# Moving keys, queries, a pool unit and a gate unit to other places of an attention loop that fills its waits with matmuls

## The chip, the cores and the metric

The kernel runs on one core of one Trainium2 chip. The metric is device time in microseconds (us) of one execution; lower is better. Five engines work beside one another, each in the order in which the program was written: PE (TensorE, matmuls), DVE (VectorE), ACT (ScalarE), POOL (GpSimd) and SP (SyncE, which here issues DMAs). An engine that waits for another one's result holds up all that is queued behind it on the same engine.

## The reference

One layer of an encoder trunk on 512 tokens of width 1024, in fp32:

```python
xn = rmsnorm(h, norm_mix[l])
proj = xn @ w_in[l]
u_s5, u_pool, qkv, gate_logits = jnp.split(proj, split_at, axis=-1)
y_s5 = s5_mixer(u_s5, ...)        # diagonal state space, both directions, GLU output
y_pool = pool_mixer(u_pool, ...)  # centred means over 2/4/8/16 tokens minus self, grouped linear
y_attn = dilated_attention(qkv)   # 16 heads of 64, three dilated windows merged, ALiBi
gates = jax.nn.sigmoid(gate_logits).reshape(bsz, L, N_BRANCHES, D_MODEL)
merged = (gates[:, :, 0] * (y_s5 @ w_branch_s5[l])
          + gates[:, :, 1] * (y_pool @ w_branch_pool[l])
          + gates[:, :, 2] * (y_attn @ w_branch_attn[l]))
h = h + merged @ w_out[l]
hn = rmsnorm(h, norm_mlp[l])
h = h + jnp.square(jax.nn.relu(hn @ w_up[l])) @ w_down[l]
```

A last rmsnorm follows. Queries, keys and values of all heads, the pool inputs and the gate logits are 128-column slices of the same product `xn @ w_in`, so they depend on nothing but the normed input and may be computed in many orders.

## The kernel before

**Matmuls.** Every large product is done with three matmuls of 128x512 per 128-row slice of the contraction: `mm3` (L121 to L123) multiplies the high part of a weight by the high and the low part of the input, and the low part of the weight by the high part of the input. A `unit_quanta` is one 128-column slice of output: 8 quanta of three matmuls into one PSUM bank (called `ps`), then a `done` function that takes the bank out. Weights arrive by DMA (`raw`), ACT rounds them to the high part `wh` (L96), and DVE subtracts for the low part `wl` (L103); this is done ahead, one unit at first and two in the stage after attention.

**Order.** Nothing reorders at run time. The order of each engine is that of the Python program: `tick()` is called after each quantum and runs what `later(n, f)` put off, and generators that `start` put in the background, which give a few instructions per tick. So where a unit stands in the list decides where all that hangs on it stands.

**Attention.** Nine steps i of eight slots s. In a slot PE does four transposes (L795) of the softmax output of head 2(i-1)+s//4, then one quantum of `main`, a tick, a second quantum of `main`, and the two score matmuls (L764, L765) of a row block of head 2i+s//4. `main` is other work that fills the time. Behind a score block DVE adds the bias and takes the maximum (L768), ACT takes the exponential (L775), and once per head DVE takes the reciprocals of the sums (L779) and POOL divides, four instructions (L109 on POOL, `S<-S,sm`). The transposes of a head need that division. `k_done` and `q_done` write a new key or query unit: two heads each, ACT copies and a DVE subtraction (L103 with 64x512 for a key, L106 for a query). POOL and DVE also make the weights of the S5 layer (`W_gen`, 64x64 matmuls at L832).

**The scan.** `s5_scan` is the S5 recurrence: 63 steps of four small POOL instructions (`st<-XS,A` twice, `st<-st`, `XS<-XS,st`). It starts in step 5, slot 3, of attention, and each step needs the one before it.

**After attention.** Stage C1 is eight rounds m of a gate unit (its `done` is a tanh on ACT, L1015) and a branch unit. At m = 6 (`V_UNIT`) `s5_script` starts: four ACT copies out of the scan's result (L96, `z<-XS`), products on DVE, four more copies and products, and then `kq`, 32 small matmuls at L1096, inside the gate unit of m = 7. The stages C2, C3, the output projection and the MLP follow.

The profile's L96, L103, L106 and L109 are helpers (`copy`, `tt`, `stt`, `ts`); the names of the tiles tell the uses apart.

Of the kernel before, what the change touches and what calls it, by code (L numbers as in the profile page):

```python
# [13 lines left out]
AF = mybir.ActivationFunctionType  # L14
# [41 lines left out]
def trunk(ctx: ExitStack, tc: tile.TileContext, a: dict, out):  # L56
    nc = tc.nc
    VE, SE, GE, TE, SP = nc.vector, nc.scalar, nc.gpsimd, nc.tensor, nc.sync
# [17 lines left out]
    def z(dt=F32, n=512):  # L76
        t = z_p.tile([128, 512], dt, tag="z", name="z")
        return t if n == 512 else t[:, 0:n]

    def zr():  # L80
        return z(F32R)

    def ps():
        return ps_p.tile([128, 512], F32, tag="ps", name="ps")
# [9 lines left out]
    def copy(eng, o, i, scale=1.0):  # L94
        if eng is SE:
            SE.activation(out=o, in_=i, func=AF.Copy, scale=scale)  # L96
        elif scale != 1.0:
            eng.tensor_scalar(out=o, in0=i, scalar1=scale, scalar2=1.0, op0=MUL, op1=MUL)
        else:
            eng.tensor_copy(out=o, in_=i)  # L100

    def tt(o, i, j, op, eng=None):
        (eng or VE).tensor_tensor(out=o, in0=i, in1=j, op=op)  # L103
# [15 lines left out]
    def mm3(o, wh, wl, xh, xl, first, last):  # L119

        TE.matmul(o, wh, xh, start=first, stop=False)  # L121
        TE.matmul(o, wh, xl, start=False, stop=False)  # L122
        TE.matmul(o, wl, xh, start=False, stop=last)  # L123
# [8 lines left out]
    def later(n, f):  # L132
        clock[1] += 1
        put_off.append((clock[0] + n, clock[1], f))

    def tick():
        clock[0] += 1
        due = sorted(x for x in put_off if x[0] <= clock[0])
        if due:
            put_off[:] = [x for x in put_off if x[0] > clock[0]]  # L140
            for _, _, f in due:
                f()
        for b in background:
            if b[0] <= clock[0]:
                try:
                    b[0] = clock[0] + (next(b[1]) or 1)
                except StopIteration:
                    b[0] = None
        background[:] = [b for b in background if b[0] is not None]
# [8 lines left out]
    def run(qs):  # L158
        for q in qs:
            q()  # L160
            tick()
# [7 lines left out]
    def add_piece(src, kind="w"):  # L169
        pieces.append((src, kind))  # L170
        if kind != "s":
            loaded.append(len(pieces) - 1)
        return len(pieces) - 1
# [61 lines left out]
    def use(i):  # L235

        j = i + 1
        while j < len(pieces) - 1 and pieces[j][1] == "z":
            j += 1
        d = SPLIT_AT  # L240
        if state["deep"] or "s" in [kind for _, kind in pieces[i:i + 3]]:
            j, d = i + 2, 1
        while state["split"] <= min(j, len(pieces) - 1):
            hi, lo = split_ops()
            later(d, hi)
            later(d + 1, lo)
            d += 3
        return splits[i]

    def cols(w, c0, n=128):  # L250

        return w[:, c0:c0 + n].rearrange("(k p) f -> p k f", p=128)
# [4 lines left out]
    w_in, w_out, w_up, w_down = a["w_in"], a["w_out"], a["w_up"], a["w_down"]  # L257
    C_POOL, C_Q, C_K, C_V, C_G = 512, 1024, 2048, 3072, 4096
# [2 lines left out]
           for hf in range(2)]  # L261
    P_s5 = [add_piece(cols(w_in, 128 * j)) for j in range(3)]
    P_qk = []
    for i in range(8):
        if i == 1:
            P_s5.append(add_piece(cols(w_in, 384)))
        P_qk.append((add_piece(cols(w_in, C_K + 128 * i)), add_piece(cols(w_in, C_Q + 128 * i))))
    P_pool = [add_piece(cols(w_in, C_POOL + 128 * j)) for j in range(4)]
    P_c1 = [(add_piece(cols(w_in, C_G + 2048 + 128 * m)), add_piece(cols(a["w_branch_attn"], 128 * m))) for m in range(8)]
    P_c2, P_c3 = [], []  # L270
    for lst, off, w in ((P_c2, 1024, a["w_branch_pool"]), (P_c3, 0, a["w_branch_s5"])):
        for m in range(0, 8, 2):
            g = [add_piece(cols(w_in, C_G + off + 128 * (m + i))) for i in range(2)]
# [24 lines left out]
    for x in range(8):  # L298
        i, hf = x // 2, x % 2
# [79 lines left out]
    xT_h, xT_l = [xh_[:, k] for k in range(8)], [xl_[:, k] for k in range(8)]  # L379
# [293 lines left out]
    def unit_quanta(pi, hT, lT, done, ks=range(8), sub=None):  # L673

        box = {}
        q = []
        n = len(ks)

        def quantum(i):
            if i == 0:  # L680
                box["w"] = use(pi)
                box["p"] = ps()
            hs, ls = box["w"]
            wh, wl = hs[i], ls[i]
            if sub is not None:
                wh, wl = wh[:, sub], wl[:, sub]
            mm3(box["p"], wh, wl, hT[ks[i]], lT[ks[i]], i == 0, i == n - 1)
            if i == n - 1:
                done(box["p"])

        return [lambda i=i: quantum(i) for i in range(n)]
# [31 lines left out]
    def k_done(i):  # L723
        def f(p):
            def part_(b):
                h = 2 * i + b
                u, o = slice(64 * b, 64 * b + 64), slice(64 - 64 * b, 128 - 64 * b)
                kh = khh[h] = zr()
                kl = kll[h] = kz[b][i % 2]
                copy(SE, kh[u], p[u])  # L730
                copy(SE, kh[o], p[u])
                later(1, lambda: tt(kl[u], p[u], fr(kh[u]), SUB))
            part_(0)
            later(2, lambda: part_(1))
        return f

    def q_done(i):
        def f(p):
            def part_(b):
                h = 2 * i + b  # L740
                u, o = slice(64 * b, 64 * b + 64), slice(64 - 64 * b, 128 - 64 * b)
                qs = qst[h] = zr()
                copy(SE, qs[u], p[u], 0.125)
                stt(qs[o], p[u], 0.125, fr(qs[u]), MUL, SUB)
            part_(0)
            later(2, lambda: part_(1))
        return f
# [56 lines left out]
    def av(i):  # L804

        p = ps()
        for kt in range(4):
            for b in range(2):
                h = 2 * i + b
                c = h % 8 * 64  # L810
                TE.matmul(p[64 * b:64 * b + 64], vt[kt][h // 8][:, c:c + 64], pts.pop((h, kt)),  # L811
                          start=kt == 0, stop=kt == 3)
        h, l = yT_h[i], yT_l[i] = zr(), zr()
        copy(SE, h, p)
        later(1, lambda: tt(l, p, fr(h), SUB))
# [46 lines left out]
    def pool_u_done(g):  # L862
        def f(p):
            upool.append(z())
            copy(SE, upool[g], p)
        return f
# [85 lines left out]
    qs = unit_quanta(P_s5[3], xT_h, xT_l, s5_u_done(3))  # L952
# [6 lines left out]
    load_T(1)  # L959
    W_load(0)  # L960
    run(qs[4:])
    for i in range(9):
        main = []
        if i < 7:
            main += unit_quanta(P_qk[i + 1][0], xT_h, xT_l, k_done(i + 1))
            main += unit_quanta(P_qk[i + 1][1], xT_h, xT_l, q_done(i + 1))
        else:
            for g in (0, 1) if i == 7 else (2, 3):
                main += unit_quanta(P_pool[g], xT_h, xT_l, pool_u_done(g))
        for s in range(8):  # L970
            if s % 4 == 0:
                W_load(2 * i + s // 4 + 1 - W_DELAY)
                W_ops(2 * i + s // 4 - W_DELAY)
            if 2 * i + s // 4 == 8 + W_DELAY and s % 4 == 3:
                start(s5_scan())
            if i >= 1:
                t_quantum(2 * (i - 1) + s // 4, s % 4)()
            main[2 * s]()
            tick()
            main[2 * s + 1]()  # L980
            if i < 8:
                s_quantum(2 * i + s // 4, s % 4)()
                if s in (3, 7) and 2 * i + 2 + s // 4 < H:
                    load_T(2 * i + 2 + s // 4)
            if s in (2, 6):
                W_mm(2 * i + s // 4 - 1 - W_DELAY)
            if s == 2 and i >= 2:
                av(i - 2)
            tick()
    av(7)  # L990
    att_p.release()
    kz_p.release()
# [13 lines left out]
    acc = {}  # L1006
    w3_p = tc.alloc_tile_pool(name="w3", bufs=1, side="right", reuse_waits="tile")
    state["wide"], state["deep"] = w3_p, True

    def gate(pi):  # L1010
        box = {}

        def done(p):
            box["th"] = z()
            SE.activation(out=box["th"], in_=p, func=AF.Tanh, scale=0.5)  # L1015
        return box, unit_quanta(pi, xT_h, xT_l, done)

    def branch_done(box, m, stage):
        def f(p):
# [224 lines left out]
    for m in range(8):  # L1244
        if m == V_UNIT - 1:
            V_load(0)
        if m == V_UNIT:
            start(s5_script())
        box, qs = gate(P_c1[m][0])
        run(qs)  # L1250
        run(unit_quanta(P_c1[m][1], yT_h, yT_l, branch_done(box, m, 0)))

    for stage, P, yh, yl in ((1, P_c2, ypool_h, ypool_l), (2, P_c3, ys_h, ys_l)):
        for n, (gs, b) in enumerate(P):
# [3 lines left out]
            for pi in gs:  # L1258
                box, qs = gate(pi)
# [68 lines left out]
    for t in range(4):  # L1328
# [3 lines left out]
        p = tok_inner(P_wo[1], mh, ml, t, mid)  # L1332
# [183 lines left out]
    for t in range(3):  # L1516
        p = tok_inner(P_dn3[1], aT_h, aT_l, t)
# [15 lines left out]
    for q in range(2):  # L1533
        p = ps()
# [91 lines left out]
```

## Time and profile before

| what | value |
|---|---|
| median of 3 runs | 942.47 us (941.71 to 943.56) |
| the profiled execution, its own time | 941.8 us |
| its span, first to last instruction | 940.0 us |
| PE busy | 918.0 us, 98% |
| DVE, ACT, POOL busy | 585.0 us (62%), 444.7 us (47%), 307.5 us (33%) |
| mean granted TensorE clock | 0.994 of full speed |

The profile is of one execution whose own time is 941.8 us; 1.8 us of that lie outside the span. Its times are given in microseconds from the start of the span. An idle time in a row is the time that the engine stood still before the instruction; "<-" names the engine, tile and line that ended the wait.

### The profile page before, as it was taken

To read this page: it belongs to the slowest core of one execution; us is meant where nothing else is said; L and a number is where in the kernel's file an instruction comes from. 1 tells how busy PE (TensorE), PEld (TensorE's weight loads), DVE (VectorE), ACT (ScalarE), POOL (GpSimd) and SP (SyncE) were. 2 spreads that over 40 slices of the span, in tenths; PEclk is the share of its full clock that TensorE was granted. 3 is DMA by queue.
4 is the path that set the end of the run, shared out by engine and by line. 5 is a ranking of instruction groups with operands and counts; after the bars stand their busy time and mean duration, and the time that the engine had idled before them with its cause. 6 is when DMAs were issued, how large, how long until landed. Compare 5 with 4: busy or idle time off the path is not lost.

```text
span 940.0 us, 12763 instructions
## 1 busy us (share of the span) xinstructions
PE 918.0 (98%) x4683; PEld 736.2 (78%) x4683; DVE 585.0 (62%) x921; ACT 444.7 (47%) x711; POOL 307.5 (33%) x416
## 2 busy tenths in 40 slices
PE   8999999999999999999989999999999999999997
PEld 6778777677777888887878888888888888888876
DVE  4698787886645655668554454436665857675443
ACT  5544765566654324555333233346444444444522
POOL 0000466556788882021010000056134314511302
PEclk9999999999999999999989999999999999999999
DMA  9237766633213334444512245271333124221222
GB/s 327 80 120 200 202 181 179 164 102 106 85 45 104 90 107 130 114 130 106 154 46 73 85 162 173 68 259 55 98 116 123 50 93 157 83 67 45 67 90 90
DMA packets 140462, 111.05 MB, mean 118 GB/s; under 512 B 16368, under 2 KB 117104, under 8 KB 140400
## 3 DMA queue, kind: packets, MB, share of 16 engines
q1 hardware_dynamic: 140400, 110.24, 39.2%
q8 instruction: 37, 0.61, 0.3%
q14 instruction: 25, 0.20, 0.1%
HBM read 106.32 MB, written 3.90 MB: 117 GB/s over the span
## 4 chain that ended last, share of the span: by engine, by line
PE 79%; DVE 13%; ACT 3%; issue 2%; DMA 1%; SPq 0%; POOL 0%; POOLq 0%; DVEq 0%; ACTq 0%
PE ps L122 20%; PE ps L121 20%; PE ps L123 20%; PE ps L1453 4%; PE ps L1451 4%; PE ps L1452 4%; DVE z L103 4%; DVE wl L103 2%; PE ps L811 2%; DVE z L106 2%; DVE S L768 2%; PE ps L795 2%; ACT z L96 1%; PE ps L1129 1%; ACT wh L96 1%
## 5 line engine op out<-in xcount | busy, mean ns | idle before, releaser
L103 DVE TENSOR_TENSOR wl<-raw,wh 128x1024 fp32r<-128x1024 f32 (+1 forms) x113 | 151.8, 1345 | 164.8 <-ACT wh L96 164.1
L121 PE MATMUL ps<-xh,wh 128*128 128x512 f32 x384 | 156.5, 408 | 0.2 <-ACT wh L96 0.2
L123 PE MATMUL ps<-xh,wl 128*128 128x512 f32 x384 | 150.7, 392 | 0.9 <-DVE wl L103 0.9
L122 PE MATMUL ps<-xl,wh 128*128 128x512 f32 x384 | 150.2, 391 | 0.0
L96 ACT ACTIVATE wh<-raw 128x1024 fp32r<-128x1024 f32 (+1 forms) x112 | 117.5, 1049 | 31.0 <-issue 8.8
L96 ACT ACTIVATE z<-ps 128x512 f32<-128x512 f32 (+4 forms) x128 | 72.8, 579 | 65.3 <-PE ps L123 25.6
L122 PE MATMUL ps<-hl,wh 128*128 128x512 f32 (+1 forms) x272 | 102.5, 377 | 0.3 <-DVE hl L103 0.3
L121 PE MATMUL ps<-hh,wh 128*128 128x512 f32 (+1 forms) x272 | 102.5, 377 | 0.2 <-ACT hh L96 0.2
L123 PE MATMUL ps<-hh,wl 128*128 128x512 f32 (+1 forms) x272 | 102.4, 376 | 0.0
L109 POOL TENSOR_SCALAR S<-S,sm 128x512 f32<-128x512 f32 x64 | 60.7, 965 | 97.3 <-ACT wh L96 78.1
L123 PEld LDWEIGHTS ps<-xh,wl 128*128 128x128 f32 x384 | 72.4, 188 | 17.1 <-DVE wl L103 1.3
L121 PEld LDWEIGHTS ps<-xh,wh 128*128 128x128 f32 x384 | 72.7, 189 | 14.8 <-PE ps L811 0.8
L122 PEld LDWEIGHTS ps<-xl,wh 128*128 128x128 f32 x384 | 72.7, 189 | 12.9
L103 POOL TENSOR_TENSOR z<-z 128x512 f32<-128x512 f32 x24 | 37.6, 1580 | 134.4 <-DVE z L106 42.4
L1352 ACT ACTIVATE R<-ps 128x512 f32<-128x512 f32 x32 | 19.2, 599 | 128.0 <-PE ps L123 128.0
L775 ACT ACTIVATE S<-S,sm 128x512 f32<-128x512 f32 x64 | 46.2, 722 | 52.6 <-DVE sm L109 50.8
L1451 PE MATMUL ps<-wh,ah 128*128 128x512 f32 x168 | 65.4, 389 | 0.0
L1452 PE MATMUL ps<-wh,al 128*128 128x512 f32 x168 | 65.4, 389 | 0.0
L1453 PE MATMUL ps<-wl,ah 128*128 128x512 f32 x168 | 65.4, 389 | 0.0
L103 POOL TENSOR_TENSOR B<-B,B 128x1024 f32<-128x1024 f32 x18 | 50.6, 2827 | 27.7 <-DVE wl L103 19.6
L122 PEld LDWEIGHTS ps<-hl,wh 128*128 128x128 f32 x272 | 51.2, 188 | 9.9 <-DVE hl L103 0.5
L121 PEld LDWEIGHTS ps<-hh,wh 128*128 128x128 f32 x272 | 51.2, 188 | 9.8 <-ACT hh L96 0.5
(208 smaller groups left out, 1850.1 us busy)
## 6 DMA issues: line engine op xcount, KB each, us to landing
raw<-in_w_in_dram SPq DMA_DIRECT2D x55, 512.0 KB
raw<-in_w_up_dram SPq DMA_DIRECT2D x32, 512.0 KB
B<-in_w_down_dram SPq DMA_DIRECT2D x24, 512.0 KB
T<-in_ttab_dram SPq DMA_DIRECT2D x16, 448.0 KB
z<-Fd SPq DMA_DIRECT2D x16, 256.0 KB
raw<-in_w_branch_attn_dram SPq DMA_DIRECT2D x8, 512.0 KB
raw<-in_w_out_dram SPq DMA_DIRECT2D x8, 512.0 KB
raw<-in_w_down_dram SPq DMA_DIRECT2D x8, 512.0 KB
```

Of the source, the lines that this page charges most:

```text
L96: SE.activation(out=o, in_=i, func=AF.Copy, scale=scale)
L103: (eng or VE).tensor_tensor(out=o, in0=i, in1=j, op=op)
L106: VE.scalar_tensor_tensor(out=o, in0=i, scalar=s, in1=j, op0=op0, op1=op1)
L109: (eng or VE).tensor_scalar(out=o, in0=i, scalar1=s1, scalar2=s2, op0=op0, op1=op1)
L121: TE.matmul(o, wh, xh, start=first, stop=False)
L122: TE.matmul(o, wh, xl, start=False, stop=False)
L123: TE.matmul(o, wl, xh, start=False, stop=last)
L775: SE.activation(out=s, in_=s, func=AF.Exp, bias=nm, accum_out=den[h][:, t:t + 1])
L1352: SE.activation(out=r, in_=p, func=AF.Relu)
L1451: TE.matmul(acc[t], ah[:, k, o], hs[i], start=st, stop=False, **kw)
L1452: TE.matmul(acc[t], al[:, k, o], hs[i], start=False, stop=False, **kw)
L1453: TE.matmul(acc[t], ah[:, k, o], ls[i], start=False, stop=sp, **kw)
```

## The change

All units of queries and keys, and those that fill the loop, are put into one list, and its first eight quanta, the key unit 1, are run before step 0. So step i takes, in slots 0 to 3, query unit i+1, and in slots 4 to 7 key unit i+2, where before it took key unit i+1 and then query unit i+1. Pool unit 0 is run whole between step 0 and step 1, without scores or transposes in between. Step 6 takes query unit 7 and pool unit 1, step 7 pool units 2 and 3, and step 8 (no scores left) only the gate unit of m = 0, in slots 0 to 3. C1 therefore begins with the branch unit of m = 0. The order in which weights are loaded (`add_piece`) follows the order of the units. What is computed stays the same.

```diff
+    k = add_k(1)
+    for i in range(1, 8):
+        q = add_q(i)
+        if i < 7:
+            k_next = add_k(i + 1)
+        P_qk.append((k, q))
+        k = k_next
         if i == 1:
-            P_s5.append(add_piece(cols(w_in, 384)))
-        P_qk.append((add_piece(cols(w_in, C_K + 128 * i)), add_piece(cols(w_in, C_Q + 128 * i))))
-    P_pool = [add_piece(cols(w_in, C_POOL + 128 * j)) for j in range(4)]
+            add_u(0)
+    for j in range(1, 4):
+        add_u(j)
...
+    units = []
+    for i in range(1, 8):
+        units += unit_quanta(P_qk[i][0], xT_h, xT_l, k_done(i))
+        units += unit_quanta(P_qk[i][1], xT_h, xT_l, q_done(i))
+    for g in range(1, 4):
+        units += unit_quanta(P_pool[g], xT_h, xT_l, pool_u_done(g))
+    gate0 = gate(P_c1[0][0])
+    units += gate0[1]
+    run(units[:8])
     for i in range(9):
-        main = []
-        if i < 7:
-            main += unit_quanta(P_qk[i + 1][0], xT_h, xT_l, k_done(i + 1))
-            main += unit_quanta(P_qk[i + 1][1], xT_h, xT_l, q_done(i + 1))
-        else:
-            for g in (0, 1) if i == 7 else (2, 3):
-                main += unit_quanta(P_pool[g], xT_h, xT_l, pool_u_done(g))
+        main = units[16 * i + 8:16 * i + 24]
...
-            main[2 * s]()
+            if main:
+                main.pop(0)()
             tick()
-            main[2 * s + 1]()
+            if main:
+                main.pop(0)()
...
+        if i == 0:
+
+            run(unit_quanta(P_pool[0], xT_h, xT_l, pool_u_done(0)))
...
-        box, qs = gate(P_c1[m][0])
+        box, qs = gate(P_c1[m][0]) if m else (gate0[0], [])
```

PE at the end of attention, before: the last transposes of step 8, two quanta of a pool unit, the last values product (eight matmuls that multiply the softmax output, `z`, by the values), and the gate unit of m = 0 (its input tiles are `xh`, `xl`).

```order
L795 MATMUL ps<-ident,S 128x128 x4
L121 MATMUL ps<-xh,wh 128x512
L122 MATMUL ps<-xl,wh 128x512
L123 MATMUL ps<-xh,wl 128x512
L121 MATMUL ps<-xh,wh 128x512
L122 MATMUL ps<-xl,wh 128x512
L123 MATMUL ps<-xh,wl 128x512
L811 MATMUL ps<-z 64x512 x8
L121 MATMUL ps<-xh,wh 128x512
```

The same place in the changed kernel: the two quanta are the end of the gate unit of m = 0, and the branch unit of m = 0 (input `z`) follows the values product.

```order
L814 MATMUL ps<-ident,S 128x128 x4
L121 MATMUL ps<-xh,wh 128x512
L122 MATMUL ps<-xl,wh 128x512
L123 MATMUL ps<-xh,wl 128x512
L121 MATMUL ps<-xh,wh 128x512
L122 MATMUL ps<-xl,wh 128x512
L123 MATMUL ps<-xh,wl 128x512
L814 MATMUL ps<-ident,S 128x128 x16
L830 MATMUL ps<-z 64x512 x8
L121 MATMUL ps<-z,wh 128x512
```

What moved: the last four slots have transposes alone, all sixteen in a row, and the eight quanta of the gate unit that stood behind the values product stand ahead of them.

DVE in step 2, slots 4 and 5, in which the odd head's first score blocks come and the even head's reciprocals (`sm<-sm 128x4`), before. The key unit that ended in slot 3 is split there (`kz`).

```order
L768 ISA S,sm<-ps,T 128x512
L768 ISA sm 128x1
L109 TENSOR_SCALAR sm<-sm 128x1
L103 TENSOR_TENSOR kz_95<-ps,z 64x512
L103 TENSOR_TENSOR z<-z 128x512
L768 ISA S,sm<-ps,T 128x512
L768 ISA sm 128x1
L109 TENSOR_SCALAR sm<-sm 128x1
L103 TENSOR_TENSOR kz_97<-ps,z 64x512
L779 RECIPROCAL sm<-sm 128x4
```

The same slots in the changed kernel, where it is the query unit that ended in slot 3 (L106 writes the low part of a query behind an ACT copy of its high part).

```order
L106 SCALAR_TENSOR_TENSOR z<-ps,z 64x512
L787 ISA S,sm<-ps,T 128x512
L787 ISA sm 128x1
L109 TENSOR_SCALAR sm<-sm 128x1
L106 SCALAR_TENSOR_TENSOR z<-ps,z 64x512
L103 TENSOR_TENSOR z<-z 128x512
L787 ISA S,sm<-ps,T 128x512
L787 ISA sm 128x1
L109 TENSOR_SCALAR sm<-sm 128x1
L798 RECIPROCAL sm<-sm 128x4
```

What moved: the query's two subtractions stand ahead of an even head's reciprocals, where the key's stood; the key's now stand ahead of an odd head's.

ACT at m = 6, before, with the semaphores that each instruction waits for (tanh of a gate unit, two weight roundings, the copies out of the scan's result, tanh, a weight rounding).

```order
L1015 ACTIVATE z<-ps 128x512 [waits PE_49]
L96 ACTIVATE wh<-raw 128x1024 [waits DMAHW0_49,Activation_49]
L96 ACTIVATE wh<-raw 128x1024 [waits DMAHW1_49,DVE_49,PE_49]
L96 ACTIVATE z<-XS 64x4x63 [waits Pool_49]
L96 ACTIVATE z<-XS 64x4x63 x3
L1015 ACTIVATE z<-ps 128x512 [waits PE_49]
L96 ACTIVATE wh<-raw 128x1024 [waits DMAHW6_49,DVE_49]
```

The changed kernel:

```order
L986 ACTIVATE z<-ps 128x512 [waits PE_49]
L96 ACTIVATE wh<-raw 128x1024 [waits DMAHW0_49,Activation_49]
L96 ACTIVATE wh<-raw 128x1024 [waits DMAHW1_49,PE_49,Activation_49]
L96 ACTIVATE z<-XS 64x4x63 [waits Pool_49]
L96 ACTIVATE z<-XS 64x4x63 x3
L986 ACTIVATE z<-ps 128x512 [waits PE_49]
L96 ACTIVATE wh<-raw 128x1024 [waits DMAHW6_49,DVE_49]
```

Nothing moved among these rows; the first copy waits for POOL's last write of the scan in both. What moved is PE's work ahead of them: sixteen quanta fewer lie between the scan's start and this place.

## Rows read from the trace of the kernel before

**Rows 1.** The page, part 1: busy time of each engine, share, instructions.

```profile
PE 918.0 (98%) x4683; PEld 736.2 (78%) x4683; DVE 585.0 (62%) x921; ACT 444.7 (47%) x711; POOL 307.5 (33%) x416
```

**Rows 2.** Timeline of PE, step 1: start, duration, instruction, idle before and releaser.

```profile
...
103.13 0.27 PE L795 MATMUL ps<-ident,S 128*128 128x128 f32 x1
...
105.08 0.47 PE L121 MATMUL ps<-xh,wh 128*128 128x512 f32 x1
...
107.02 0.60 PE L795 MATMUL ps<-ident,S 128*128 128x128 f32 x4
107.37 0.47 PE L121 MATMUL ps<-xh,wh 128*128 128x512 f32 x1
...
113.88 0.38 PE L795 MATMUL ps<-ident,S 128*128 128x128 f32 x2
...
115.62 0.48 PE L121 MATMUL ps<-xh,wh 128*128 128x512 f32 x1
```

**Rows 3.** Groups by line on PE, 80:300: count, busy, mean ns, idle before, releaser.

```profile
...
L795 PE MATMUL ps<-ident,S 128*128 128x128 f32 x256 | 40.6, 276 | 2.4 <-POOL S L109 2.4
...
L764 PE MATMUL ps<-z 128*128 128x512 f32 x64 | 25.6, 399 | 1.6 <-DVE z L106 1.5
```

**Rows 4.** Timeline of DVE, around the splits of a key and of a query.

```profile
...
167.17 0.69 DVE L768 CUSTOM_DVE_ANT_0 S<-ps,T 128x512 f32<-128x512 f32 x1
...
171.38 0.18 DVE L779 RECIPROCAL sm<-sm 128x4 f32<-128x4 f32 x1
...
178.73 0.69 DVE L768 CUSTOM_DVE_ANT_0 S<-ps,T 128x512 f32<-128x512 f32 x1
...
183.84 0.17 DVE L779 RECIPROCAL sm<-sm 128x4 f32<-128x4 f32 x1
```

**Rows 5.** Timeline of POOL and PE, even heads: end of the division, start of the transposes.

```profile
...
145.54 4.63 POOL L109 TENSOR_SCALAR S<-S,sm 128x512 f32<-128x512 f32 x4
...
150.28 0.60 PE L795 MATMUL ps<-ident,S 128*128 128x128 f32 x4
...
196.64 4.62 POOL L109 TENSOR_SCALAR S<-S,sm 128x512 f32<-128x512 f32 x4 [0.97 <-ACT wh L96]
...
201.24 0.60 PE L795 MATMUL ps<-ident,S 128*128 128x128 f32 x4
```

**Rows 6.** Timeline of POOL, the scan: first, after the last division, slowed, last.

```profile
...
212.79 0.60 POOL L103 TENSOR_TENSOR st<-XS,A 128x64 f32<-128x64 f32 x2
...
276.51 0.59 POOL L103 TENSOR_TENSOR st<-XS,A 128x64 f32<-128x64 f32 x2
...
295.07 1.94 POOL L103 TENSOR_TENSOR st<-XS,A 128x64 f32<-128x64 f32 x2
...
358.94 0.33 POOL L103 TENSOR_TENSOR XS<-XS,st 128x64 f32<-128x64 f32 x1
```

**Rows 7.** Timeline of PE, ACT and DVE around the start of m = 6.

```profile
...
359.62 0.39 PE L121 MATMUL ps<-xh,wh 128*128 128x512 f32 x1
...
374.68 1.08 PE L1096 MATMUL ps<-z,Bb 128*32 128x128 f32 x32
...
360.56 2.69 ACT L96 ACTIVATE z<-XS 64x252 f32<-64x252 f32 x4
365.26 0.60 ACT L1015 ACTIVATE z<-ps 128x512 f32<-128x512 f32 x1 [2.00 <-PE ps L123]
365.88 1.06 ACT L96 ACTIVATE wh<-raw 128x1024 fp32r<-128x1024 f32 x1
...
366.98 1.23 DVE L103 TENSOR_TENSOR wl<-raw,wh 128x1024 fp32r<-128x1024 f32 x1 [1.58 <-ACT wh L96]
...
373.65 0.69 DVE L103 TENSOR_TENSOR z<-z 128x512 f32<-128x512 f32 x1
```

**Rows 8.** Timeline of PE, the end of its longest stall.

```profile
...
476.15 0.79 PE L122 MATMUL ps<-z 128*128 128x512 f32 x1 [1.99 <-DVE z L103]
```

**Rows 9.** Windows, right behind that: busy (count) by engine, PE's granted clock, DMA share, GB/s.

```profile
core 0: us, PE busy (x) PEld busy (x) DVE busy (x) ACT busy (x) POOL busy (x), PEclk, DMA share, GB/s
476.20:482.30 6.10, 6.10 (x15) 4.75 (x16) 1.88 (x3) 1.23 (x2) 0.00 (x0) 0.50 0.29 89
```

More of the change, by code (lines that the diff above doesn't have):

```diff
@@ L263, in trunk, with add_k, add_q, add_u @@
     P_qk = []
-    for i in range(8):
+    P_pool = []
+    def add_k(i):
+        return add_piece(cols(w_in, C_K + 128 * i))
+    def add_q(i):
+        return add_piece(cols(w_in, C_Q + 128 * i))
+    def add_u(j):
+        P_pool.append(add_piece(cols(w_in, C_POOL + 128 * j)))
+    P_qk.append((add_k(0), add_q(0)))
+    P_s5.append(add_piece(cols(w_in, 384)))
+    k = add_k(1)
[5 more added lines that the diff above has]
+        k = k_next
         if i == 1:
-            P_s5.append(add_piece(cols(w_in, 384)))
-        P_qk.append((add_piece(cols(w_in, C_K + 128 * i)), add_piece(cols(w_in, C_Q + 128 * i))))
-    P_pool = [add_piece(cols(w_in, C_POOL + 128 * j)) for j in range(4)]
+            add_u(0)
+    for j in range(1, 4):
+        add_u(j)
     P_c1 = [(add_piece(cols(w_in, C_G + 2048 + 128 * m)), add_piece(cols(a["w_branch_attn"], 128 * m))) for m in range(8)]
@@ L961, in trunk, with gate, done @@
     run(qs[4:])
-    for i in range(9):
-        main = []
-        if i < 7:
-            main += unit_quanta(P_qk[i + 1][0], xT_h, xT_l, k_done(i + 1))
-            main += unit_quanta(P_qk[i + 1][1], xT_h, xT_l, q_done(i + 1))
-        else:
-            for g in (0, 1) if i == 7 else (2, 3):
-                main += unit_quanta(P_pool[g], xT_h, xT_l, pool_u_done(g))
+    def gate(pi):
+        box = {}
+        def done(p):
+            box["th"] = z()
+            SE.activation(out=box["th"], in_=p, func=AF.Tanh, scale=0.5)
+        return box, unit_quanta(pi, xT_h, xT_l, done)
+    units = []
[7 more added lines that the diff above has]
+    run(units[:8])
+    for i in range(9):
+        main = units[16 * i + 8:16 * i + 24]
         for s in range(8):
@@ L1008, in trunk @@
     state["wide"], state["deep"] = w3_p, True
[L1010 to L1016, printed above, removed]
     def branch_done(box, m, stage):
```

## The prediction

> **What bounds the kernel now.** I read the page's busy times first: PE works 98% of the span [rows 1], so the kernel is matmul time plus the few places where PE waits, and an order with the same matmuls can move only those places. The groups by line over attention name two of them: transposes wait for POOL's division, 2.4 us in all, and scores wait for the query's subtraction on DVE, 1.6 us [rows 3]. Then I looked for engines that finish something just in time, since a shift uses up that time. The timeline has one in the middle: the S5 scan on POOL, whose last write ends at 358.94 + 0.33 = 359.27 [rows 6], while the stage that needs it, m = 6, starts on PE at 359.62 and on ACT, with the copies out of the scan, at 360.56 [rows 7]. I take that place to decide.
>
> **The change, part by part.** The matmuls are the same, so their sum is nothing.
>
> *Step 1's transposes, removed wait.* The group that begins at 103.13 is followed by the next matmul at 105.08, 1.95 us later; an undisturbed group takes 107.37 - 107.02 = 0.35 [rows 2]. That is 1.60. The second, 113.88 to 115.62, is 1.74, so 1.39 too long. Pool unit 0 puts 24 matmuls between step 0's last scores and the transposes. One matmul's pitch is 15.06/66 = 0.228 us (359.62 to 374.68, two whole units and six quanta) [rows 7], so the cover is 5.5 us, more than the first wait. The second, of the odd head, has its last scores ahead of that unit too. Both go: **-3.0**; -1.6 if only the first does.
>
> *Queries ahead, removed wait.* A query unit now ends four slots before its scores instead of right before them. The 1.6 us [rows 3] go: **-1.6**, and nothing is late in its place on PE, since a slot holds eight matmuls and four transposes, and the split takes DVE and ACT some 5 us at most [rows 4].
>
> *The query's split now meets the even heads.* What the split delays is not the scores alone: DVE takes its instructions in order, and behind the two subtractions stand the reciprocals of a head, behind them POOL's division, behind that the transposes. With a key's split among them, DVE went from a score block to the reciprocals in 171.38 - 167.17 = 4.21; with a query's it took 183.84 - 178.73 = 5.11 [rows 4], since each subtraction waits for an ACT copy. One more subtraction stands ahead of that stretch, 0.69 like any 512-wide DVE instruction [rows 7]. Together 0.90 + 0.69 = 1.6 us later for an even head. Those have no time left: a division ends at 145.54 + 4.63 = 150.17 and its transposes begin at 150.28; another ends at 196.64 + 4.62 = 201.26, and they begin at 201.24 [rows 5]. Such groups stand at the start of steps 2 to 5 before the scan, four of them. Upper bound 4 x 1.6 = 6.4; lower bound 0, since the division at 196.64 followed an ACT instruction and not the reciprocals [rows 5], so another chain may set its start. I take the two groups that the rows show without margin: **+3.2**.
>
> What these three change comes before the scan's start and moves all that follows: -1.4.
>
> *The scan loses cover.* From 212.79, when it starts, to 276.51, when the last division is done, POOL alternates between divisions and scan steps; then 41 steps fill it to 359.27, (359.27 - 276.51)/41 = 2.02 us each, without idle of note [rows 6]. POOL is the limit there and PE's order doesn't hasten it. But between the scan's start and m = 6 the changed kernel has 16 quanta less: queries, keys and pool units run eight quanta earlier, pool unit 0 is ahead too. That is 48 x 0.228 = 10.9 us less on PE. Before, the scan ended 0.35 us ahead of m = 6; now it ends 10.9 - 0.35 = 10.6 behind it. ACT waits there, and behind its copies stand a tanh and the roundings of weights that PE is to use; behind those DVE's subtractions, which stand ahead of the last sum for `kq`.
>
> *How much of that PE feels.* Counted from ACT's first copy: four copies 2.69, tanh 0.60, rounding 1.06, so 4.35; DVE's low part 1.23 gives 5.6; then two products, a sum and the gated product of m = 6 on DVE, 4 x 0.65 = 2.6 (0.69 each less the overlap), two more products 1.3, gives 9.5; another low part and the last sum, 1.23 + 0.69, gives 11.4, less overlap, 11.2 [rows 7]. ACT's second copies and next rounding (2.69 + 1.06, to 8.1) lie beside that. So `kq` can start 10.6 + 11.2 = 21.8 us after m = 6 starts. PE gets there 374.68 - 359.62 = 15.06 after it [rows 7], with weights that were split before ACT stopped. Stall: **+6.7**. Bounds: 4.5, if the scan speeds up by a us (DVE stands still, too) and the chain is a us shorter; 9, if the products on DVE slow the scan and the chain is a us longer.
>
> That the scan's instructions can be slowed by something, two rows show: a pair of multiplications takes 0.59 at 276.51 and 1.94 at 295.07 [rows 6]. [...]
>
> *The clock behind the stall.* [...] The new stall is longer: **+2.7**, and 0 as the lower bound if the next wait covers it. [...]
>
> *Hidden edits.* Step 8's bare transposes and the early tanh cost nothing: the same instructions, and what waits for attention's last output, the branch unit of m = 0, is followed by the scan's wait, which swallows a delay of up to 6.7 us. The order of weight loads follows the units; weights are split a unit ahead as before.
>
> **Sum**, against the profiled execution's own 941.8: -3.0 - 1.6 + 3.2 + 6.7 + 2.7 = +8.0, 949.8. The median of the runs shown is 0.7 above that execution: 950.5.
>
> **Rivals.** A measurement of this kernel can tell about 0.2%, 1.9 us, from no change.
>
> *The waits go and the scan is covered (faster).* The even heads bear the query's split, and the scan is done in time. Price: -4.6, so 942.5 - 4.6 = 937.9. It decides this way where ACT's copies start less than 15.06 - 11.2 = 3.9 us after m = 6, that is, where the 41 steps take 6.7 us less, 1.86 instead of 2.02 each. For it: unhindered steps are shorter (0.59 for a pair that took 1.94 elsewhere). [...] Or the chain to `kq` has slack that I don't see.
>
> *Gains and stall cancel (no change).* The attention gains stay at -4.6, the stall is at its lower bound 4.5 with little of the clock's cost: 942.5 - 4.6 + 4.5 = 942.4, up to 944.4.
>
> *The even heads are hit harder.* All four groups wait, 6.4, the stall is 9: 942.5 - 4.6 + 6.4 + 9 + 2.7 = 956.0. Buffers of `z` that come free late could do it; no row here says that they do.
>
> **How the numbers follow.** The forecast, a stall at m = 6 that outweighs attention's gain, 0.74, with its own range from 944.4 to 955.5; faster 0.14 (937.9, and all below 940.6); no change 0.08 (940.6 to 944.4); the harder hit 0.04. The predicted time is the forecast's, 950.5. The range from 942.0 to 955.5 leaves out the faster case and the harder one, 0.18, and a small part of no change. Faster 0.14, same 0.08, slower 0.78.
>
> **What would show it.** Right: step 1's transposes in 0.35 each; no idle at the score line; 41 or so steps of the scan behind the last division at about 2 us; ACT's first copy out of the scan about 10 us after m = 6 starts; PE idle 5 to 9 us ahead of `kq` or of the weights just ahead of it, then matmuls at half clock. The scan's start would be early by 1.4 and its length, 146.5, as before. Wrong: the scan's steps come out at 1.9 us or less, PE doesn't wait at m = 6, or the transposes of even heads show waits of more than 6 us, or none.

## The result: 16.7 us slower

The changed kernel takes 959.68 us (median of 4 runs, 956.85 to 960.26), the kernel before 943.01 beside it (4 runs): a ratio of 1.0167, 95% interval 1.0144 to 1.0191. The prediction was 950.5 with a range up to 955.5. The side and the place that was to decide, the late scan, were right. The loss is twice the forecast, and most of the difference lies in attention, where a gain of 1.4 us was expected. The profiled execution took 959.22 with a span of 957.4, which is 17.4 us more than the 940.0 of the kernel before.

Timeline of PE in the changed kernel, step 1 (columns as in [rows 2]):

```profile
114.70 0.60 PE L814 MATMUL ps<-ident,S 128*128 128x128 f32 x4
115.93 0.50 PE L121 MATMUL ps<-xh,wh 128*128 128x512 f32 x1 [0.63 <-ACT wh L96]
...
117.19 0.50 PE L123 MATMUL ps<-xh,wl 128*128 128x512 f32 x1 [0.53 <-DVE wl L103]
```

The four transposes run in one piece, so the wait of [rows 2] is gone. But the weights behind them are not ready: ACT's rounding, which starts at 114.83, stands in ACT's queue behind exponentials that waited for DVE (0.59 us ahead of 108.04 and 1.18 ahead of 110.03) and behind copies. The wait has changed its place more than its size.

Groups by line on PE over attention, 90:303 (columns as in [rows 3]; L814 are the transposes, L783 the scores, L851 the 64x64 matmuls of the S5 weights):

```profile
L814 PE MATMUL ps<-ident,S 128*128 128x128 f32 x256 | 41.8, 279 | 6.1 <-POOL S L109 5.9
...
L783 PE MATMUL ps<-z 128*128 128x512 f32 x64 | 25.6, 400 | 0.0
...
L851 PE MATMUL ps<-z 128*64 128x64 f32 x256 | 9.6, 226 | 0.7 <-DVE z L103 0.7
```

Against [rows 3]: the scores' 1.6 us went to 0, as forecast; the transposes' wait for the division grew from 2.4 to 6.1. Since step 1 no longer has a part in it, the growth in the later steps is from 0.5 to 6.1.

Where it grew, at the start of step 5, as a timeline of DVE, POOL and PE:

```profile
211.18 0.69 DVE L787 CUSTOM_DVE_ANT_0 S<-ps,T 128x512 f32<-128x512 f32 x1
...
214.05 0.69 DVE L106 SCALAR_TENSOR_TENSOR z<-ps,z 64x512 fp32r<-64x512 f32 x1 [1.98 <-ACT z L96]
...
216.28 0.17 DVE L798 RECIPROCAL sm<-sm 128x4 f32<-128x4 f32 x1
...
216.65 4.44 POOL L109 TENSOR_SCALAR S<-S,sm 128x512 f32<-128x512 f32 x4 [6.77 <-DVE sm L798]
...
218.70 0.33 PE L814 MATMUL ps<-ident,S 128*128 128x128 f32 x1
219.37 0.33 PE L814 MATMUL ps<-ident,S 128*128 128x128 f32 x1 [0.34 <-POOL S L109]
220.47 0.33 PE L814 MATMUL ps<-ident,S 128*128 128x128 f32 x1 [0.77 <-POOL S L109]
221.14 0.33 PE L814 MATMUL ps<-ident,S 128*128 128x128 f32 x1 [0.34 <-POOL S L109]
```

From the score block at 211.18 to the reciprocals it is 5.10 us, the same 5.11 that [rows 4] show for a query's split, now ahead of an even head. POOL, idle for 6.77, starts on the reciprocals at once, and PE takes each transpose as it is fed.

Behind two such groups of waits, at the starts of steps 4 and 5, TensorE's granted clock fell to 0.50 of full speed. Two windows of the changed kernel, and the last of e4, a run below that has the same program to the end of attention (columns as in [rows 9]):

```profile
190.90:194.20 3.30, 3.30 (x9) 2.51 (x9) 3.27 (x8) 2.03 (x6) 0.00 (x0) 0.50 0.89 222
221.60:225.00 3.40, 3.40 (x11) 2.61 (x10) 3.35 (x9) 2.39 (x6) 0.00 (x0) 0.50 0.14 27
...
190.50:193.80 3.30, 3.30 (x18) 2.73 (x19) 3.27 (x8) 2.13 (x6) 0.00 (x0) 1.00 0.83 212
```

e4 kept the full clock at this place, behind the same four waits. The twelve matmuls that begin at 190.76 in the changed kernel take 3.86 us, and the same twelve 2.29 in e4, so a stretch like this costs 1.6. In the kernel before the clock is never at half in attention (1.00 from 103.1 to 268.9). Attention, from the first transposes of step 1 to those of step 8, took 174.8 us instead of 165.8. Of these 9.0, 4.2 are idle time of PE (8.2 instead of 4.0) and some 3.2 the two stretches at half clock, an estimate from the 1.6. The 1.6 that are left go with transposes that come one at a time (0.33 each, where four in a row take 0.60).

But DVE was late already. In step 4, ACT and DVE, timeline:

```profile
199.68 0.60 ACT L96 ACTIVATE z<-ps 128x512 f32<-128x512 f32 x1 [5.77 <-PE ps L851]
...
201.53 0.69 DVE L103 TENSOR_TENSOR kz<-ps,z 64x512 fp32r<-64x512 f32 x1 [6.18 <-ACT z L96]
```

ACT wants to copy transposes out of PSUM and has no data to wait for (the last of them were done at 197.2): the matmuls at L851 on PE read a buffer of `z`, and ACT gets it when they are done. DVE stands behind ACT for 6.18. In the kernel before, DVE's longest wait in attention is 2.82, and no term of the prediction stands for a wait like this one.

Then the scan, timeline of POOL, ACT and PE (L1124 is `kq`):

```profile
231.73 0.60 POOL L103 TENSOR_TENSOR st<-XS,A 128x64 f32<-128x64 f32 x2 [0.87 <-DVE XS L100]
...
380.80 0.33 POOL L103 TENSOR_TENSOR XS<-XS,st 128x64 f32<-128x64 f32 x1
...
381.15 2.66 ACT L96 ACTIVATE z<-XS 64x252 f32<-64x252 f32 x4 [11.16 <-POOL XS L103]
...
368.91 0.39 PE L121 MATMUL ps<-xh,wh 128*128 128x512 f32 x1
...
383.97 0.43 PE L1124 MATMUL ps<-z,Bb 128*32 128x128 f32 x8
388.77 1.08 PE L1124 MATMUL ps<-z,Bb 128*32 128x128 f32 x16 [4.38 <-DVE z L103]
392.31 0.65 PE L1124 MATMUL ps<-z,Bb 128*32 128x128 f32 x8 [2.46 <-DVE z L103]
```

m = 6 starts at 368.91; ACT's first copy comes 12.2 us later (forecast 10.6), after 11.16 us in which ACT stood still. `kq` is reached at 383.97, which is 15.06 after the start, as before to the hundredth. Its matmuls, 0.8 us from the first start to the last in the kernel before, take from 383.97 to 392.54, 7.8 us more.

Windows at the end of that stall and behind it (columns as in [rows 9]):

```profile
388.80:392.30 3.50, 1.05 (x16) 0.58 (x16) 3.45 (x5) 0.32 (x1) 0.00 (x0) 0.50 0.27 95
392.30:395.40 3.10, 3.09 (x14) 2.23 (x15) 0.57 (x3) 0.63 (x2) 0.00 (x0) 0.50 0.61 176
395.40:398.50 3.10, 3.10 (x14) 2.49 (x14) 1.09 (x1) 2.65 (x4) 0.00 (x0) 0.96 0.17 38
```

The clock is at half from 388.8 to 395.6, 6.8 us, of which the first 3.5 lie inside the stall. (In the kernel before it is at half from 475.5 to 482.3, as long, but nearly all of it behind the stall, which ended at 476.15.) PE was 17.2 us behind the kernel before when `kq` ended (392.89 against 375.69), and 18.5 behind it afterwards (494.67 against the 476.15 of [rows 8]): the half clock behind the stall cost 1.3. Behind the later stall the changed kernel then had less of the half clock than [rows 9] (0.73 in 494.7 to 500.8 against 0.50), which gave back 1.1. What is left is 17.4.

### The profile page after: what moved, and what is told of

Same layout as the page of the kernel before. It is cut to its first block, busy times and chain, and to the rows that moved or that the text cites. A ratio compares the mean times of both kernels' runs of the same rounds, so it can differ in the third digit from the quotient of the medians.

```text
span 957.4 us, 12772 instructions
## 1 busy us (share of the span) xinstructions
PE 924.2 (97%) x4683; PEld 739.7 (77%) x4683; DVE 591.4 (62%) x921; ACT 444.8 (46%) x711; POOL 305.4 (32%) x416
## 4 chain that ended last, share of the span: by engine, by line
PE 66%; POOL 12%; DVE 10%; issue 4%; ACT 3%; DMA 3%; SPq 1%; POOLq 0%; DVEq 0%; ACTq 0%
PE ps L122 16%; PE ps L123 16%; PE ps L121 16%; POOL st L103 7%; PE ps L1481 4%; PE ps L1479 4%; PE ps L1480 4%; DVE z L103 3%; POOL XS L103 2%; DVE wl L103 2%; POOL S L109 2%; DVE z L106 2%; ACT z L96 2%; DMA z<-in_s_bq_im_dram 1%; PE ps L814 1%
## 5 line engine op out<-in xcount | busy, mean ns | idle before, releaser
L103 DVE TENSOR_TENSOR wl<-raw,wh 128x1024 fp32r<-128x1024 f32 (+1 forms) x113 | 160.9, 1425 | 170.0 <-ACT wh L96 169.1
L103 POOL TENSOR_TENSOR z<-z 128x512 f32<-128x512 f32 x24 | 35.1, 1472 | 139.4 <-DVE z L106 81.1
L103 DVE TENSOR_TENSOR z<-z 128x512 f32<-128x512 f32 (+1 forms) x68 | 52.0, 772 | 11.1 <-ACT z L96 7.4
```

## The experiments

A few starts, of the profiled executions, tell the stages apart. "Attention" is from the first transposes of step 1 to those of step 8. "Copy" is ACT's first copy out of the scan, counted from the start of the S5 stage, which is 15.06 us ahead of the first `kq` matmul (66 matmuls, undisturbed in all runs); "kq" is the time from the first to the last start of its 32 matmuls, 0.8 to 1.1 undisturbed. The ratio is to the kernel before, run on the same chip beside it. The edits are against the changed kernel, those of e5 and e13 against the kernel before.

| kernel | ratio (95%) | attention | scan ends | copy | kq |
|---|---|---|---|---|---|
| before | | 165.8 | 359.3 | 0.9 | 0.8 |
| changed | 1.0167 (1.0144 to 1.0191) | 174.8 | 381.1 | 12.2 | 8.6 |
| e1 half step alone | 1.0056 (1.0035 to 1.0077) | 169.8 | 371.8 | 7.4 | 3.7 |
| e2 pool unit alone | 1.0057 (1.0037 to 1.0076) | 170.1 | 373.7 | 7.4 | 3.7 |
| e3 late split | 1.0072 (1.0052 to 1.0092) | 164.7 | 370.6 | 12.2 | 8.6 |
| e4 script one unit later | 1.0132 (1.0106 to 1.0157) | 172.9 | 378.2 | 0.9 | 0.8 |
| e5 before, 37 buffers | 1.0043 (1.0028 to 1.0058) | 170.2 | 364.3 | 0.9 | 0.8 |
| e6 pool unit not kept | 1.0039 (1.0023 to 1.0056) | 165.7 | 368.9 | 7.4 | 3.8 |
| e7 late split, earlier scan | 1.0003 (0.9980 to 1.0026) | 165.2 | 364.6 | 6.0 | 2.2 |
| e8 half step, late split, earlier scan | 1.0023 (1.0008 to 1.0038) | 170.4 | 363.1 | 0.9 | 0.8 |
| e9 late split, buffer taken early | 1.0053 (1.0035 to 1.0071) | 163.4 | 368.9 | 12.2 | 8.5 |
| e10 half step, late split | 0.9999 (0.9984 to 1.0014) | 163.0 | 364.1 | 7.2 | 3.4 |
| e11 as e10, script later | 0.9924 (0.9907 to 0.9941) | 165.4 | 365.8 | 1.7 | 1.1 |
| e12 as e7, script later | 0.9939 (0.9924 to 0.9953) | 165.1 | 364.0 | 1.7 | 1.1 |
| e13 before, script later | 0.9962 (0.9941 to 0.9983) | 168.4 | 362.8 | 1.7 | 1.1 |
| e14 changed, script later | 1.0041 (1.0024 to 1.0059) | 172.9 | 380.1 | 7.6 | 2.7 |
| e15 as e10, 37 buffers | 1.0003 (0.9983 to 1.0023) | 165.3 | 366.5 | 7.2 | 3.5 |

The changed kernel, e4 and e14 have the same program up to the end of attention, and so do before and e13, and e10 and e11; their attention differs by 1.9, 2.6 and 2.4 us. The 1.9 is mostly one stretch at half clock: step 4 took 30.5 us in the changed kernel and 28.9 in e4 and e14. A difference below 3 us in that column means nothing by itself; where one matters, the ratios decide.

Theory 1 is the prediction's own, sized anew: the query's split in front of the even heads' reciprocals costs attention all of what it lost. Theory 2, its rival: buffers of `z` are short. Pool unit 0's result is put into one of the 38 between steps 0 and 1, and it stays there until the pool mixer runs after attention; before, the pool units' results took theirs in steps 7 and 8.

**e1**, the half-step shift alone:

```diff
-        if i == 1:
-            add_u(0)
...
-        if i == 0:
-
-            run(unit_quanta(P_pool[0], xT_h, xT_l, pool_u_done(0)))
...
-    gate0 = gate(P_c1[0][0])
-    units += gate0[1]
```

> Only the half-step shift of keys and queries; pool units 0 to 3 stay at the loop's end (step 6, slots 4 to 7, to step 8, slots 0 to 3), the gate unit of m = 0 back in C1. Theory 1, the query's split in front of the even heads' reciprocals is the loss in attention: even heads wait as in the changed kernel, attention loses about 10 us, the scan's wait shrinks to 1.5 to 3 us, time 954 to 956. Theory 2, buffers of z are short because pool unit 0's output holds one through all of attention: ACT's wait of 5.8 us for a buffer in step 3 goes, attention loses 3 us at most, time 946 to 949.

**e2**, pool unit 0 alone:

```diff
-    run(units[:8])
...
-        main = units[16 * i + 8:16 * i + 24]
+        main = units[16 * i:16 * i + 16]
```

with keys before queries as in the kernel before.

> Only pool unit 0 between steps 0 and 1; keys and queries in the order of the kernel before, gate unit of m = 0 back in C1. Theory 1: attention loses nothing against before and gains up to 3 us in step 1, the scan's wait costs 1.5 to 3 us, time 941 to 945. Theory 2: waits for z buffers appear in steps 3 to 5 and attention loses 4 to 6 us, time 947 to 951.

950.41 and 950.18 us, beside 944.87 for the kernel before: e1 lies between the ranges of the two theories, e2 in that of theory 2. Each half loses some 4 us of attention, both together 7 to 9: neither theory alone. In e1's profile only 0.5 of its 4.0 is more idle time of PE (4.5 against 4.0); most of the rest is two stretches at half clock, 112.0 to 115.4 and 211.0 to 214.4, some 3.2 by the price above. The first stands behind step 1's transposes, which this half leaves waiting, and which brought no half clock in the kernel before. e2, whose even heads have the key's split as before, should have lost nothing by theory 1. Its longest wait is in step 4, slot 2 (the expectations call it step 3); PE in it, and ACT and DVE ahead of it (L846 is the S5 matmul):

```profile
194.05 0.69 PE L846 MATMUL ps<-z 128*64 128x64 f32 x16 [2.12 <-DVE z L103]
...
191.97 0.59 ACT L96 ACTIVATE z<-ps 64x512 fp32r<-64x512 f32 x1 [3.77 <-PE ps L846]
...
192.60 0.69 DVE L106 SCALAR_TENSOR_TENSOR z<-ps,z 64x512 fp32r<-64x512 f32 x1 [5.72 <-ACT z L96]
```

ACT waits for a buffer of `z` that earlier S5 matmuls release, DVE for ACT, and the S5 matmuls for DVE.

**e3**, the late split:

```diff
-            part_(0)
-            later(2, lambda: part_(1))
+            later(5, lambda: part_(0))
+            later(6, lambda: part_(1))
```

> The changed kernel with the query's split put off by five and six ticks, so that it stands behind the even heads' reciprocals on DVE and ACT; PE's order is unchanged. Theory 1: the even heads' waits go, attention is about 10 us shorter, the wait for the scan stays, time 948 to 952. Theory 2: ACT still waits for a buffer of z that the S5 matmuls free, DVE behind it, attention is 2 to 4 us shorter, time 955 to 958.

951.55 us beside 944.87, in theory 1's range. Attention is 10.1 us shorter than in the changed kernel, at 164.7 no longer than in the kernel before, with PE's order and pool unit 0 where the change put them. The transposes' wait is 2.2 instead of 6.1, in the groups by line on PE:

```profile
L814 PE MATMUL ps<-ident,S 128*128 128x128 f32 x256 | 39.9, 277 | 2.2 <-POOL S L109 1.5 <-DVE sm L787 0.6
```

What stays is the scan: its copies come 12.2 us after m = 6, as in the changed kernel, since the scan's end and PE's work moved ahead by the same 10.5 us, and `kq` takes the same 8.6.

**e4**, the S5 stage one unit later:

```diff
-V_UNIT = 6
+V_UNIT = 7
```

> The changed kernel with the S5 stage started at m = 7 instead of m = 6. If the late scan is what PE waits for: ACT's first copy comes about 1 us after its stage starts, PE waits less than 1 us at kq, the low clock goes too, time 949 to 952. Rival, the S5 chain bounds what follows: the stall comes back further on, time 955 to 960.

956.20 us beside 944.87, in the rival's range. The wait at the first `kq` is gone, but more than half of it comes back at the three later ones, where PE idles 5.9 us in all instead of 2.2. The longest of these waits:

```profile
462.60 0.65 PE L1124 MATMUL ps<-z,Bb 128*32 128x128 f32 x8 [3.50 <-DVE z L103]
```

So the rival had a part: a stage that starts 10.9 us later is itself late further on.

**e5**, the kernel before with one buffer less, and **e6**, e2 without keeping the unit's result:

```diff
-NZ = 38
+NZ = 37
```

```diff
+            if g == 0:
+                return
             upool.append(z())
-            copy(SE, upool[g], p)
+            copy(SE, upool[g - 1], p)
...
-    copy(SE, u[:, 8:520], upool[g])
+    copy(SE, u[:, 8:520], upool[max(g - 1, 0)])
```

> The kernel before with 37 buffers of z instead of 38, nothing else. Theory 2, one buffer more or less decides in attention (pool unit 0 holds one from step 0 to the end): waits for buffers that the S5 matmuls free show up on ACT in step 3, attention is 3 to 5 us longer, time 946 to 950. If buffers are not what pool unit 0 costs: no change, 942 to 945.

> As the run with pool unit 0 alone moved, but its result is not copied out of PSUM (so it holds no buffer of z), and the pool mixer takes units 1, 1, 2, 3 in place of 0, 1, 2, 3: pool unit 0's part of the result is left out. PE's order is the same. Theory 2: step 3's waits for a buffer go, attention is about 4 us shorter than with it, time 944 to 947. If the place of the unit itself is what costs: 949 to 951, as with it.

e5 took 947.57 beside 943.75, e6 947.70, which lies between its two ranges. In the profiles, one buffer taken from the kernel before costs its attention 4.4 us (some 1.6 of it a stretch at half clock behind the wait, 187.9 to 191.3), and one buffer given back to e2 returns 4.4 (170.1 to 165.7). In time the first is clear, 3.8 us. The second is not: e6's ratio is only 0.0018 below e2's, and their intervals overlap. In the profile of e6 the clock was at half for 13.7 us between 370 and 490, in that of e2 for 3.4, and the spans end up at 948.0 and 948.4. e5 has e2's waits, at the same place and within a hundredth of the same length:

```profile
184.86 0.59 ACT L96 ACTIVATE z<-ps 64x512 fp32r<-64x512 f32 x1 [3.76 <-PE ps L832]
...
185.49 0.69 DVE L106 SCALAR_TENSOR_TENSOR z<-ps,z 64x512 fp32r<-64x512 f32 x1 [5.72 <-ACT z L96]
...
186.94 0.69 PE L832 MATMUL ps<-z 128*64 128x64 f32 x16 [2.12 <-DVE z L103]
```

In e6 the S5 matmuls of attention don't wait at all:

```profile
L846 PE MATMUL ps<-z 128*64 128x64 f32 x256 | 9.2, 225 | 0.0
```

So where the queries stay in their old place, what pool unit 0 costs attention is a buffer, and not its matmuls: the same waits come with one buffer less and go with one given back. In time only the price of e5 is measured.

**e7** and **e8**: the changed kernel, and the half-step shift alone, each with the late split and this:

```diff
-W_DELAY = 2
+W_DELAY = 1
```

> The changed kernel with the query's split put off behind the reciprocals, and with the S5 weights and the scan four slots earlier (W_DELAY = 1). If the two losses are the split among the even heads and the late scan: attention as in the run with the late split, ACT's first copy about 1 us after m = 6 starts, no wait at kq, time 940 to 944. Rival, the earlier S5 weights meet the shortage of z buffers: waits in steps 1 to 4 on ACT and POOL, time 946 to 951.

> The half-step shift alone (pool units at the loop's end) with the late split and the S5 weights and scan four slots earlier. Theory: no waits of scores or even heads, scan done 5 us ahead of m = 6; only step 1's transposes still wait 3 us; time 940 to 943. Rival: buffers of z are short with the earlier S5 weights, time 945 to 949.

942.74 and 946.82 beside 943.75. With both repairs, the changed order costs nothing: e7's interval holds 1. The wait for the scan is mostly gone, but the first copy comes 6.0 us behind m = 6, not 1, as the scan started 10 us earlier than in e3 and ran 149.9, against 145.8 there. e8 is 4 us above its range, in that of the rival: step 1 took 27.2 and step 2 27.5 us, where e10, the same without the earlier S5 weights, took 21.2 and 24.2. A stretch at half clock stands in each (111.8 to 115.2 and 139.1 to 142.5). That the earlier S5 weights fall on step 1's waits, which the shift alone doesn't remove, was not tested further.

**e9** parts the two effects of the late split, the order and the time for which buffers are held. It has e3's lines, and these:

```diff
+            qst[2 * i] = zr()
+            later(2, lambda: qst.__setitem__(2 * i + 1, zr()))
...
-                qs = qst[h] = zr()
+                qs = qst[h]
```

> As the run with the late split of the query, but the two buffers of z for the query are taken when they were taken in the changed kernel, so that only the order of the instructions differs from the changed kernel, and not how long buffers are held. If the order in front of the reciprocals is the loss: attention as with the late split, 10 us shorter than in the changed kernel, time 949 to 953. If the gain of the late split came from buffers held for a shorter time: attention 2 to 5 us shorter than in the changed kernel, waits for a buffer on ACT or POOL in step 3, time 954 to 958.

949.39 us beside 943.72; attention 163.4, 11.4 below the changed kernel, like e3, and in the range that stands for the order. The order is the loss, not the holding. **e10** is the half-step shift with the late split, **e15** the same with 37 buffers:

> The half-step shift alone, with the late split; S5 weights and scan as in the changed kernel. Attention 2 us shorter than before (scores don't wait, step 1's transposes do), the scan ends 5.5 us behind the start of m = 6, ACT's first copy 6.9 us behind it, so a wait of 6.9 - 3.9 = 3.0 us at kq: time 943 to 946.

> The half-step shift with the late split, with 37 buffers of z. If a buffer costs by itself, as in the kernel before: attention 3 to 5 us longer than with 38, 946 to 949. If it costs only where the even heads' reciprocals stand behind the query's split: 0 to 1.5 us, 943 to 945.

943.17 (beside 943.72) and 944.64 (beside 944.21). e10's attention is 163.0, and 165.4 in e11, which has the same program so far; before and e13 took 165.8 and 168.4. The scan's wait takes back what that gains. e15's time lies in the second of its ranges, and its attention, 165.3, is that of e11 with 38 buffers: with the late split, a buffer less costs nothing that the runs can tell (1.0003 against 0.9999).

The ratios also price the split's place, without leaning on single profiles: from 1.0167 to 1.0072 (e3) it cost the changed kernel 9.0 us, and from 1.0056 to 0.9999 (e10) it cost the half-step shift alone 5.4.

**e11** to **e14** start the S5 stage eight quanta later, in e10, in e7, in the kernel before and in the changed one:

```diff
-        if m == V_UNIT:
-            start(s5_script())
         box, qs = gate(P_c1[m][0])
         run(qs)
+        if m == V_UNIT:
+            start(s5_script())
```

> As the half-step shift with the late split, and the S5 stage started eight quanta later, behind the gate unit of m = 6. The wait at kq goes (ACT's first copy about 1.5 us behind the stage's start); if nothing of the S5 stage is late further on: 940 to 943. Rival: the S5 stage's later waits take the 3 us, 943 to 946.

> The changed kernel with the late split, the S5 weights and scan four slots earlier, and the S5 stage started eight quanta later. No wait at kq; attention as with the earlier scan; time 939 to 943 if nothing further on is late, 943 to 946 if the later stage costs what the wait gave.

> The kernel before with only the S5 stage started eight quanta later. If the gain of the two fast runs with the later stage comes from that stage (its later waits at the second kq and the yq are smaller and the low clock behind them goes): 3 to 5 us faster than before, 938 to 941. If it comes from the half-step shift: 942 to 945.

> The changed kernel with only the S5 stage started eight quanta later. The scan's wait is 12.1 - 5.4 = 6.7 us behind the stage's start, so 6.7 - 3.9 = 2.8 us at kq instead of 7.9, and the later waits shrink by 3 us: 949 to 953. If the loss is bound to the scan's end alone: 955 to 959.

e11 took 936.94 beside 943.72, e12 938.20 beside it, e13 940.47 and e14 948.02 beside 944.21. The ranges of e11, e12 and e14 were missed by 0.8 to 3.1 us on the fast side. e14 gets 1.26% of the changed kernel's 1.67% back, with `kq` at 2.7 instead of 8.6; the 7.6 - 3.9 = 3.7 us of wait that the prediction's chain gives are too many here (1.9 were lost), where no tanh stands between ACT's copies and the next rounding. e13 shows that the later start alone is worth 0.4%: the stall of [rows 8] is less than half as long and no half clock follows (1.00 from 480 to 486). PE in e13, and the window behind the like stall in e11:

```profile
482.90 0.50 PE L122 MATMUL ps<-z 128*128 128x512 f32 x1 [0.85 <-DVE z L103]
```

```profile
478.80:484.90 6.10, 5.24 (x22) 4.09 (x23) 3.29 (x5) 1.71 (x3) 0.00 (x0) 1.00 0.29 87
```

e11's interval ends where e13's begins, at 0.9941: the 0.0038 between the ratios would be what the half-step shift itself gives once its costs are taken away. e11 is clearly faster than the kernel before and the changed one.

## Why the prediction was right in its side and wrong in its size

*What bounds the kernel, and the scan's cover.* Right. The rule worked out from the rows, stall = (first copy behind m = 6) - 3.9, gives 8.3 for the 12.2 of the changed kernel and 3.5 for e1's 7.4; `kq` lost 7.8 and 2.9. The forecast of 10.6 was short by 1.6: the scan ran 381.1 - 231.7 = 149.4 us instead of 146.5, while PE's way from the scan's start to m = 6 shrank by 9.7 us (146.8 to 137.2) and not by 10.9. The term, 6.7, measured 7.8. Of the scan's 2.9 us, 1.7 came before the end of the last division and 1.2 in the 41 steps behind it. That stretch has 164 instructions of the scan. In the kernel before, 37 of them took 0.65 to 1.36 us, in the changed kernel 42 took 0.65 to 1.41, and each of them had a DVE instruction beside it, 20 and 19 of them a weight's subtraction (`wl<-raw,wh`). The 83 and 74 with no DVE instruction beside them took 0.31 to 0.33, and so did 44 and 48 that had one. What the slow ones took above 0.32 comes to 21.9 and 23.1 us, and the 1.2 is the difference. Lost cover alone doesn't lengthen the scan as a whole: e1, e2 and e10, which also lost cover, ran 150, 149 and 147, and e3 and e9, which had the least (133.5), 146 both.

*Clock.* Over-sized behind `kq`, and put at nothing in attention. The 2.7 was an estimate: the 6.1 us at half clock of [rows 9] less the 3.4 that their 15 matmuls take at 0.228 each. No row showed that a longer stall costs the same: here 6.8 us were at half, but half of them fell into the stall. What lay behind it measured 1.3, and 1.1 came back further on. Attention's two stretches cost some 3.2 that no term stood for. That the three make 3.4 in all, near 2.7, is luck. With attention's 9.0 in full and 7.8 at `kq`, 1.3 and -1.1 make 17.0 of the 17.4.

*Queries ahead.* Right: the score line's wait is 0.

*Step 1.* The waits for the division went, but 3.0 came out as 1.3 (step 1 took 21.2 us instead of 22.5): PE ran into weights that ACT rounds behind its exponentials (waits of 0.63 and 0.53).

*Even heads: the step that failed.* "The query's split now meets the even heads", +3.2 with a bound of 6.4. With -3.0 and -1.6 it was to make -1.4; attention lost 9.0 in the profiled execution and 7.1 in the two other profiles of the same program. The mechanism was right: 5.10 us against the forecast 5.11, and without it (e9) the whole loss goes. The size was wrong: by the ratios the split's place cost 9.0 us and not 3.2. It was counted as a fixed 1.6 us per head, without what a late head brings with it. In the changed kernel DVE comes to that stretch late, from a wait of 6.18 for ACT, which waits 5.77 for a buffer of `z`; and twice the clock fell to 0.50 behind the waits. The wait for a buffer doesn't need pool unit 0: e1 has it too, shorter (4.25 and 3.14, in step 4). The prediction named such buffers in its last rival, whose 956.0 came nearest to the result, and gave it 0.04, as no row showed them. A reader could have counted them: a result that is computed in step 0 and used after step 8 holds a buffer for all of attention, and in the trace of before POOL, which there reads and writes buffers of `z` alone, waits for the S5 matmuls to release one:

```profile
184.76 3.18 POOL L103 TENSOR_TENSOR z<-z 128x512 f32<-128x512 f32 x2 [8.42 <-PE ps L832]
```

*How the two act together.* The buffer alone costs 3.8 us of time (e5), the split 5.4 without pool unit 0 at its new place and 9.0 with it. The late split takes away the whole loss of attention though pool unit 0 still holds its buffer (e3, e9), and with it a buffer less costs nothing that the runs can tell (e15 beside e10 and e11). So they are not a sum: a buffer that comes late costs when the engines behind it have no time to spare, and the late split gives them that time. That is what the runs agree with; the exact chain from one buffer to the next was not followed, and stays open.

## What to carry to other kernels

Work that is moved ahead to fill a wait takes two things with it that the order doesn't show: the buffers that its result holds until it is used, and the cover that it gave to a slow chain at the place it left. Ask of each moved unit who was hidden behind it, and how long its output now lives. And when a producer is moved away from its consumer, look at what stands behind its last instructions in the new place: here they could be put off at no cost that the runs show, and that was worth 9 us. Short waits that stand close together can cost more than their sum, as the four of 0.34 to 0.77 us ahead of 190.76 did with the 1.6 of the half clock behind them: look at the granted clock there.

## What was not expected of the hardware and the program

One buffer of 38 is worth 3.8 us of 944 (e5). A stall of 7.8 us came with 6.8 us at half clock, and the stall of [rows 8], with two waits of 0.43 and 1.99, as many (475.5 to 482.3); the longer stall cost less clock (1.3 against 2.7), since 3.5 of its 6.8 fell into the stall itself. Four waits of 0.34 to 0.77 us ahead of 190.76 were followed by the half clock in one execution, and the same four in e4 were not. And the same program gave attention times that are 1.9 us (changed, 174.8 against 172.9) and 2.6 us (before, 165.8 against 168.4) apart between executions.
